# A hybrid attention and delta-rule layer on one core: products of probabilities and v in batches of ready blocks, and a new slab order

## The chip, the core and the metric

The kernel runs on one core of a Trainium2 chip. The core has a matrix engine (TensorE, PE in the profile), a vector engine (VectorE, DVE), a scalar engine (ScalarE, ACT), a general engine (GpSimd, POOL) and a sync engine (SyncE, SP) that issues most DMAs. Each works through its own instructions in order and waits for the others at semaphores. Matmuls read SBUF and write banks of PSUM. The metric is the device time of one execution in microseconds (us): before, the median of 3 runs is 747.47, with 744.84, 747.47 and 747.5.

## The reference

One layer of an encoder over 512 tokens of width 1024, in float32. What matters here:

```
h  = rms_norm(x)                                   # one projection of h for all that follows
q, k = rope(rms_norm(heads)); v = heads            # 8 query heads, 2 key/value heads of 128
s  = q k^T * scale;  pr = softmax(s);  o_att = pr v
y_att = (o_att * silu(az)) @ w_br_att
qkv = silu(short_conv(dq, dk, dv));  o_dn = gated delta rule, chunks of 64, forward and backward
y_dn = (rms_norm(o_dn) * silu(dz)) @ w_br_dn
mix = (sigmoid(gate_att) * y_att + sigmoid(gate_dn) * y_dn) @ w_out
x = x + rms_norm(mix)
x = x + rms_norm(sigmoid(x @ w_ple_gate) * (p @ w_ple_proj))
```

Every large product is computed with both operands split in a high part that the matrix engine takes in one pass and a low rest, and three matmuls (low x high, high x low, high x high) are added up in PSUM.

## The kernel before, in words

**Staging.** The weights come in slabs of 128 x 1024 (512 KB). ACT casts a slab to its high part (`whi`), POOL or DVE subtracts to get the low part (`wlo`; `split`, line 250), and PE runs eight steps of three 128 x 512 matmuls on it (`gemm_t`, lines 549 to 551; `gemm_n` and `gemm_k`, lines 568 to 570 and 586 to 588, for slabs on the moving side). Homes of slabs are two `wraw`, `whi` and `wlo` each, and units `u0` to `u16` lent for a time (`SPARE`). First come the projections of h in the sequence of `ORDER` (dk, dq, dv are the delta rule's; az, dz, gA, gB gates; kv, q0, q1 attention), with the delta rule's two groups of four heads beside them (`chain`), then `ydn` (branch projection of the delta rule), attention, `yatt`, `out0`, `out1`, `pg0`, `pg1`.

**Attention** (`att_heads`, line 1581) is done in two batches g of four heads. For each head and 128 queries PE makes scores (lines 1606 to 1608), DVE their maximum, ACT the exponential with the row's sum, and DVE transposes the result in blocks of 32 into `T` (unit `u0`), so that 16 blocks b of 32 keys lie on 32 partitions each. Then each block is prepared (line 1658: ACT casts the high part, DVE subtracts the low part) into a home of its own: `ring0`, `ring1` (unit `u14`) or one of three `blk` tiles. The products with v (`pv`, line 1641) are twelve matmuls for a block: three split terms times four groups a of 32 partitions, each group on 32 rows of the array with 512 columns, into four banks `po`. PE runs a block's products once more than `AHEAD` = 4 blocks are pending, and the planner may put other parts' matmuls between blocks. The second batch's `att_heads(1)` is started when the first batch's products are done. Afterwards DVE multiplies `po` with the gate, and ACT and POOL or DVE split it (lines 1691 to 1710).

**Planner.** Nothing of the order on the engines is written out by hand. `Flow` (line 36) runs the parts as generators on a clock of assumed durations. A part asks for a home ("get"), a time ("at"), an event ("ev") or PE for a duration ("pe"); of the ready parts the one with the lowest priority number goes on. Other engines' operations are recorded at the first free time that the planner sees for their engine. `W` marks a DVE operation during which the planner leaves POOL idle, too; `split` chooses POOL or DVE for a slab by their planned ends and `COOL` or `HOT`. So a change of a duration, a priority or the sequence in `ORDER` redraws the order of all engines. `PVB` is the assumed duration of a block's products, `VGAP` the distance of the loads of v, `PR` the priorities, `OUT0` the places at which slabs of `out0` are loaded.

**Late stages.** `out1_tail` (line 1867) forms the new x for 128 tokens; its last steps are a DVE product into a `whi` or `wlo` tile and PE's transposes of it (line 1888) for `pg0` and `pg1`.

Of the kernel before, what the change touches and what calls it, by code (L numbers as in the profile page):

```python
# [9 lines left out]
F32 = mybir.dt.float32  # L10
F32R = mybir.dt.float32r
# [24 lines left out]
class Flow:  # L36
# [7 lines left out]
    def __init__(self, slots):  # L44
        self.now = 0.0
        self.eng = {}
        self.slots = {k: [0.0] * n for k, n in slots.items()}
        self.parts = []
        self.later = []
        self.n = 0  # L50
        self.shut, self.link = None, lambda a, b: None

    def spawn(self, gen, prio):
        ev = Event()
        self.n += 1
        self.parts.append([prio, self.n, gen, ("at", 0.0), ev])
        return ev
# [49 lines left out]
    def free(self, tag, t=None):  # L107
        self.slots[tag].append(self.now if t is None else t)
# [15 lines left out]
    def run(self):  # L124
        while self.parts:
            best, soon = None, None
            for p in self.parts:
                r = self.ready(p[3])
                if r is None:
                    continue  # L130
                if r <= self.now + 1e-9:
                    if best is None or p[:2] < best[:2]:
                        best = p
                elif soon is None or r < soon:
                    soon = r
            if best is None:
                if soon is None:
                    raise RuntimeError("stuck: " + ", ".join(f"{p[0]} {p[2].__name__} {p[3][:2]}" for p in self.parts))
                self.now = soon
                continue  # L140
            if best[3][0] == "get":
                s = self.slots[best[3][1]]
                s.remove(min(s))
            self.flush()
            try:
                want = next(best[2])
            except StopIteration as e:
                self.parts.remove(best)
                best[4].set(max(self.now, e.value or 0.0))
                continue  # L150
            if want[0] == "pe":
                self.now += want[1]
                want = ("at", self.now)
            best[3] = want
        self.now = 1e9
        self.flush()


ORDER = """
vec dq1 dk0 dk1 dk3 dq2 dk2 dq3 dq0 dv3 dv1 az0 dq5 dq7 dv2 dq6  # L160
az5 gB7 dk5 az6 dz7 dk4 az2 gA2 dz2 gA4 gA6 dv0 gA7 dq4 dk6 gB4
dk7 gA5 gB3 az4 dz1 dv7 dv4 dz6 dz0 gB0 gB1 kv dv5 dv6 gA0 dz4
gB5 az3 az7 gB2 gA3 dz3 q0 dz5 gB6 q1 gA1 az1 free_h ydn3 ydn4 ydn2
ydn5 heads_on0 ydn6 ydn0 heads_on1 ydn1 ydn7 yatt6 yatt1 yatt5 yatt7 yatt4 yatt2 yatt3 yatt0 out0
out1 pg0 pg1
"""
OUT0 = 'yatt0 yatt3 yatt2 yatt7'
PR = dict(dec=1, dm1=11, y=7, conv=1, gate=3, kv=9, q=5, head=6, ple=7, prep=1, tab=6)
GAP = 0.0
EXPS = 0.32  # L170
SP13 = 480.0
SPARE = ((15, "raw", 7.0, 190.0), (11, "pair", 22.0, 80.0), (12, "pair", 22.0, 80.0), (14, "pair", 279.0, 375.0),
         (13, "pair", 443.0, SP13), (6, "pair", 560.0, 640.0), (14, "raw", 590.0, 640.0))
EOUT = 29.73
WIDE = 2.0
LAND = "c2"
LONG, NEAR = 0.6, 1.5
X_DVE = ()
WARM = 5.5
PVB = 0.695  # L180
VGAP = 2.0
HEADHOT = 1
AHEAD = 4
SPAREMM = 2
W1 = 0
COOL, HOT = 13.37, -0.27


@with_exitstack
def layer(ctx, tc, x, xT, pw0, wp1, wt, wba, wn, rows, qkn, hd16, npost, pnorm, dnorm, cs, out):  # L190
    nc = tc.nc
    pe, act, dve, pool, sync = nc.tensor, nc.scalar, nc.vector, nc.gpsimd, nc.sync

    caps = {"wraw": 2, "whi": 2, "wlo": 2, "f2": 5, "c2": 4, "blk": 3, "gi": 2, "go": 2, "mm": 5, "aux": 3}
    F = Flow({**caps, **{f"u{i}": 1 for i in range(17)}})
    op, free, spawn = F.op, F.free, F.spawn
# [6 lines left out]
    def A(dur, dep, fn, *a, **k):  # L203
        return op("ACT", dur, dep, fn, *a, **k)
# [4 lines left out]
    def W(dur, dep, fn, *a, **k):  # L209

        return op(("DVE", "POOL"), dur, dep, fn, *a, **k)
# [14 lines left out]
    def tile(tag, shape, dt=F32):  # L226
        cnt[0] += 1
        return sb.tile(list(shape), dt, tag=tag, bufs=caps.get(tag, 1), name=f"{tag}_{cnt[0]}")
# [95 lines left out]
    load, ple, late = {}, {}, {}  # L324
# [288 lines left out]
    def gate_job(kind, n):  # L613
        o = yield from gemm_t((kind, n))
        gate_ev[kind, n] = spawn(gate_tail(kind, n, o), PR["gate"])

# [325 lines left out]
    def r32(i):  # L942
        return slice(32 * i, 32 * i + 32)
# [562 lines left out]
    v_ev, V4 = {}, {}  # L1506
# [74 lines left out]
    def att_heads(g):  # L1581
# [6 lines left out]
        T = unit(0, [128, 16, 4, 4, 32])  # L1588
# [6 lines left out]
        def soonest(*tags):  # L1595
            return min(tags, key=lambda n: min(F.slots[n], default=1e9))

        tT = 0.0
        for hb in range(4):
            h = 4 * g + hb  # L1600
            for t in range(NT):
# [17 lines left out]
                tT = V(0.64, te, dve.transpose, T[:, :, hb, t, :], P)  # L1619
# [6 lines left out]
            free(f"u{u}")  # L1626
        if g == 1:
            free("u6")
        yield "ev", v_ev[g]
        yield "ev", q_ev[1]  # L1630
        if g == 1:
            weighed.set(F.now)
        po = []
# [4 lines left out]

        chains[0] += HEADHOT

        def pv(b, p):
            v = V4[g][b // 8][:, b % 8]
            for i, j in ((1, 0), (0, 1), (0, 0)):
                for a in range(4):
                    pe.matmul(po[a], v[r32(a), i, :], p[r32(a), j], start=(b == 0 and i == 1), stop=(b == 15 and i + j == 0))  # L1645
            free(tag[b], F.now + PVB + 0.1)

        yield "get", "u14"
        ring = unit(14, [128, 2, 2, 16, 32], F32R)
        for i in range(2):  # L1650
            F.slots[f"ring{i}"] = [F.now]
        pend, tag = [], {}
        for b in range(16):
            tag[b] = soonest("ring0", "ring1", "blk")
            yield "get", tag[b]
            p = tile("blk", [128, 2, 16, 32], F32R) if tag[b] == "blk" else ring[:, int(tag[b][-1])]
            w = T[:, b].rearrange("p h t q -> p (h t) q")
            tl = W(0.58, A(0.52, tT, act.copy, p[:, 0], w), dve.tensor_sub, p[:, 1], w, p[:, 0].bitcast(F32))
            pend.append((b, p, tl))
            if len(pend) > AHEAD:  # L1660
                b_, p_, t_ = pend.pop(0)
                yield "at", t_ + 0.3
                pv(b_, p_)
                yield "pe", PVB
        free("u0", tl)
        for b_, p_, t_ in pend:
            yield "at", t_ + 0.3
            pv(b_, p_)
            yield "pe", PVB
        for u in (15, 13):  # L1670
            free(f"u{u}")
        chains[0] -= HEADHOT
# [2 lines left out]
        free("u14")  # L1675
        if g == 0:
            v_ev[1] = spawn(v_rows(1), 4)
            spawn(att_heads(1), PR["head"])
        us = ((9, 10), (11, 12))[g]
        for u in us:  # L1680
            yield "get", f"u{u}"
# [9 lines left out]
        for a in range(4):  # L1691
            if g == 0:
                yield "get", "c2"
                y = tile("c2", [128, 16, 32])
                t = V(0.66, max(tz), dve.tensor_mul, y, po[a], at(uz))
# [3 lines left out]
                t = G(1.19, th, pool.tensor_sub, at(ya[g][1]), y, at(ya[g][0]).bitcast(F32))  # L1699
# [4 lines left out]
        if g == 1:  # L1704
            half_ev.set(th + 0.2)
            for a in range(4):
                t = V(0.58, th, dve.tensor_sub, at(ya[g][1]), po[a], at(ya[g][0]).bitcast(F32))
# [318 lines left out]
    dec = spawn(decay(), PR["dec"])  # L2026
# [41 lines left out]
    for j in jobs:  # L2068
        f, a = j[0], tuple(j[1:])
# [86 lines left out]
```

## Time and profile before

| | |
|---|---|
| median of 3 runs | 747.47 us (744.84 to 747.5) |
| profiled execution | 745.96 us |
| its span, first to last instruction | 744.2 us |
| granted TensorE clock, mean | 0.996 |
| PE busy | 729.0 us, 98% |
| DVE, ACT, POOL busy | 495.3, 348.8, 304.1 us |
| DMA moved | 118.49 MB, mean 159 GB/s |
| first batch of products (L1645) | 533.2 to 549.4 us of the span |
| second batch of products | 579.4 to 602.0 us |

The page gives busy time by engine, the chain of work that ended last, and the costliest groups of instructions. A matmul's duration runs from its start to its modelled end and overlaps the next one's; what PE needs for a matmul is the distance from its start to the next start. Waits are put down to the engine and tile whose signal came last. The profile's line numbers are those of the code above.

### The profile page before, as it was taken

What the parts mean: (1) busy time and instruction counts of PE and PEld (TensorE: products, weight loads), DVE (VectorE), ACT (ScalarE), POOL (GpSimd) and SP (SyncE); (2) the same over time, 40 slices, a digit from 0 to 9 for tenths busy, and PEclk for the clock granted to TensorE, in tenths of its full rate; (3) what the DMA queues carried; (4) which work ended last, traced back from release to release, by engine and by line L of the source; (5) the groups of instructions that cost most, each with busy time, mean ns of one, the idle gap of its engine ahead of it and who ended that gap; (6) DMA issues with size and microseconds to landing.
All of it is one profiled execution on the core that took longest, in us unless ns stands there. A gap on an engine that the chain in (4) does not pass through costs nothing.

```text
span 744.2 us, 12250 instructions
## 1 busy us (share of the span) xinstructions
PE 729.0 (98%) x4601; PEld 600.7 (81%) x4601; DVE 495.3 (67%) x912; ACT 348.8 (47%) x647; POOL 304.1 (41%) x292
## 2 busy tenths in 40 slices
PE   8999999999999999999999999999999999999995
PEld 7788888888788988887888988888777578887885
DVE  4688989898776668878734537368878863315434
ACT  6657674553643535425532254335656634322422
POOL 5836494211431444125411257454325218372501
PEclk9999999999999999999999999999999999999998
DMA  8774446966530235647431333475556477461323
GB/s 350 249 235 118 165 136 184 309 196 211 133 99 31 84 130 155 213 157 184 151 107 43 102 112 104 165 184 187 185 129 201 156 264 247 135 216 58 103 69 113
DMA packets 74731, 118.49 MB, mean 159 GB/s; under 512 B 23920, under 2 KB 39216, under 8 KB 74672
## 3 DMA queue, kind: packets, MB, share of 16 engines
q1 hardware_dynamic: 74384, 117.45, 49.6%
q8 instruction: 36, 0.59, 0.3%
q10 hardware_dynamic: 288, 0.26, 0.1%
q14 instruction: 23, 0.19, 0.1%
HBM read 93.41 MB, written 24.28 MB: 158 GB/s over the span
## 4 chain that ended last, share of the span: by engine, by line
PE 80%; DVE 8%; ACT 4%; DMA 3%; POOL 3%; issue 2%; POOLq 0%; DVEq 0%; SPq 0%; ACTq 0%
PE mm L549 14%; PE mm L550 14%; PE mm L551 14%; PE mm L570 4%; PE mm L568 4%; PE mm L569 4%; DVE f L122 3%; PE aux L1645 3%; PE mm L588 2%; PE mm L586 2%; PE mm L587 2%; PE aux L1218 2%; PE aux L1250 2%; PE aux L1236 2%; PE aux L1198 1%
## 5 line engine op out<-in xcount | busy, mean ns | idle before, releaser
L549 PE MATMUL mm<-u,wlo 128*128 128x512 f32 x488 | 197.2, 404 | 1.3 <-POOL wlo L102 0.9
L102 POOL TENSOR_TENSOR wlo<-wraw,whi 128x1024 fp32r<-128x1024 f32 x47 | 112.5, 2394 | 208.3 <-ACT whi L122 197.2
L551 PE MATMUL mm<-u,whi 128*128 128x512 f32 x488 | 190.4, 390 | 0.0
L550 PE MATMUL mm<-u,whi 128*128 128x512 f32 x488 | 190.2, 390 | 0.0
L549 PEld LDWEIGHTS mm<-u,wlo 128*128 128x128 f32 x488 | 91.8, 188 | 23.8 <-issue 4.0
L551 PEld LDWEIGHTS mm<-u,whi 128*128 128x128 f32 x488 | 91.6, 188 | 19.6
L550 PEld LDWEIGHTS mm<-u,whi 128*128 128x128 f32 x488 | 91.9, 188 | 16.4
L122 ACT CAST whi<-wraw 128x1024 fp32r<-128x1024 f32 x62 | 64.9, 1047 | 68.7 <-PE mm L551 28.3
L122 DVE SCALAR_TENSOR_TENSOR f<-mm,cw,f 128x510 f32<-128x510 f32 (+1 forms) x96 | 71.4, 745 | 6.6 <-ACT f L122 4.1
L568 PE MATMUL mm<-u,u 128*128 128x512 f32 (+1 forms) x136 | 52.0, 382 | 0.0
L570 PE MATMUL mm<-u,u 128*128 128x512 f32 (+1 forms) x136 | 51.3, 377 | 0.0
L569 PE MATMUL mm<-u,u 128*128 128x512 f32 (+1 forms) x136 | 51.2, 377 | 0.0
L102 POOL TENSOR_TENSOR u<-wraw,u 128x1024 fp32r<-128x1024 f32 x17 | 40.6, 2400 | 21.1 <-ACT u L122 21.0
L122 DVE TENSOR_TENSOR u<-aux,u 128x512 f32<-128x512 f32 (+2 forms) x55 | 36.1, 667 | 17.5 <-ACT u L122 11.7
L122 ACT COPY c<-aux 128x512 f32<-128x512 f32 x18 | 10.6, 587 | 48.1 <-DVE f L122 26.0
L586 PE MATMUL mm<-whi,u 128*128 128x512 f32 x80 | 31.8, 398 | 0.0
L588 PE MATMUL mm<-whi,u 128*128 128x512 f32 x80 | 31.2, 390 | 0.0
L587 PE MATMUL mm<-wlo,u 128*128 128x512 f32 x80 | 31.1, 389 | 0.0
L122 ACT ACTIVATE mm<-f 128x512 f32<-128x512 f32 x24 | 14.4, 600 | 32.2 <-DVE f L122 32.0
L570 PEld LDWEIGHTS mm<-u,u 128*128 128x128 f32 x136 | 25.6, 188 | 4.8
L569 PEld LDWEIGHTS mm<-u,u 128*128 128x128 f32 x136 | 25.6, 188 | 4.5
L568 PEld LDWEIGHTS mm<-u,u 128*128 128x128 f32 x136 | 25.6, 188 | 4.4
(286 smaller groups left out, 1499.9 us busy)
## 6 DMA issues: line engine op xcount, KB each, us to landing
wraw<-in_wt_dram SPq DMA_DIRECT2D x58, 512.0 KB, 3.7
wraw<-in_wn_dram SPq DMA_DIRECT2D x24, 512.0 KB, 4.4
u<-in_wt_dram SPq DMA_DIRECT2D x14, 512.0 KB, 5.9
u<-CI SPq DMA_DIRECT2D x16, 256.0 KB, 5.6
u<-VD SPq DMA_DIRECT2D x16, 256.0 KB, 6.8
u<-in_x_dram SPq DMA_DIRECT2D x4, 512.0 KB, 5.9
u<-in_xT_dram SPq DMA_DIRECT2D x4, 512.0 KB, 8.2
eD<-u SPq DMA_DIRECT2D x8, 256.0 KB, 5.0
```

Source lines behind the costliest of these rows:

```text
L102: ins = fn(*a, **k)
L122: fn(*a, **k)
L549: pe.matmul(o, lo[:, k, :], mh(k), start=(k == 0), stop=False)
L550: pe.matmul(o, hi[:, k, :], ml(k), start=False, stop=False)
L551: pe.matmul(o, hi[:, k, :], mh(k), start=False, stop=(k == 7))
L568: pe.matmul(o, b, hi, start=(i == 0), stop=False)
L569: pe.matmul(o, a, lo, start=False, stop=False)
L570: pe.matmul(o, a, hi, start=False, stop=(i == 7))
L586: pe.matmul(o[t], b, hi, start=(k == 0), stop=False)
L587: pe.matmul(o[t], a, lo, start=False, stop=False)
L588: pe.matmul(o[t], a, hi, start=False, stop=(k == 7))
L1645: pe.matmul(po[a], v[r32(a), i, :], p[r32(a), j], start=(b == 0 and i == 1), stop=(b == 15 and i + j == 0))
```

## The change

1. The products of a batch begin when up to `BATCH` = 4 blocks are ready (or all that are pending), and go on with the next block without giving PE away if that block is ready by the planner's clock; a visit that comes back from other work is planned `TURN` = 0.3 longer. `Flow.steps` counts PE requests, so that a part sees whether another one had PE in between. `AHEAD` goes.
2. A block may also live in two `c2` tiles, when at least two are free: with four `c2` tiles that makes seven homes instead of five.
3. `att_heads(1)` is started when the first batch's last block is prepared, and `v_ev` is polled, since the second batch's loads of v may not be spawned yet.
4. `ORDER`, `OUT0`, the priorities `PR`, `VGAP` (2.0 to 1.2), `EOUT` and `HOT` have new values.

```
@@ ORDER and constants
-vec dq1 dk0 dk1 dk3 dq2 dk2 dq3 dq0 dv3 dv1 az0 dq5 dq7 dv2 dq6
...
-ydn5 heads_on0 ydn6 ydn0 heads_on1 ydn1 ydn7 yatt6 yatt1 yatt5 yatt7 yatt4 yatt2 yatt3 yatt0 out0
+dq2 dk1 dk2 dk0 dq3 dk3 dq0 dq1 dv3 az4 dv1 dv2 dk4 az0 dq7 dq5
...
+ydn5 heads_on0 ydn1 ydn7 ydn0 ydn4 yatt1 yatt6 yatt2 yatt4 yatt0 yatt3 yatt5 heads_on1 yatt7 out0
-OUT0 = 'yatt0 yatt3 yatt2 yatt7'
-PR = dict(dec=1, dm1=11, y=7, conv=1, gate=3, kv=9, q=5, head=6, ple=7, prep=1, tab=6)
+OUT0 = 'yatt3 yatt4 yatt0 yatt5'
+PR = dict(dec=3, dm1=1, y=9, conv=1, gate=9, kv=3, q=3, head=9, ple=9, prep=1, tab=9)
-EOUT = 29.73
+EOUT = 29.88
-VGAP = 2.0
+VGAP = 1.2
-AHEAD = 4
+BATCH, TURN = 4, 0.3
-COOL, HOT = 13.37, -0.27
+COOL, HOT = 13.37, 0.47
@@ Flow.run
             if want[0] == "pe":
                 self.now += want[1]
+                self.steps += 1
@@ att_heads
+        while g not in v_ev:
+            yield "at", F.now + 1.0
         yield "ev", v_ev[g]
...
-        pend, tag = [], {}
-        for b in range(16):
-            tag[b] = soonest("ring0", "ring1", "blk")
-            yield "get", tag[b]
-            p = tile("blk", [128, 2, 16, 32], F32R) if tag[b] == "blk" else ring[:, int(tag[b][-1])]
-            w = T[:, b].rearrange("p h t q -> p (h t) q")
-            tl = W(0.58, A(0.52, tT, act.copy, p[:, 0], w), dve.tensor_sub, p[:, 1], w, p[:, 0].bitcast(F32))
-            pend.append((b, p, tl))
-            if len(pend) > AHEAD:
-                b_, p_, t_ = pend.pop(0)
-                yield "at", t_ + 0.3
-                pv(b_, p_)
-                yield "pe", PVB
-        free("u0", tl)
-        for b_, p_, t_ in pend:
-            yield "at", t_ + 0.3
-            pv(b_, p_)
-            yield "pe", PVB
+        def room():
+            ways = [(min(F.slots[n], default=1e9), n) for n in ("ring0", "ring1", "blk")]
+            if len(F.slots["c2"]) > 1:
+                ways.append((sorted(F.slots["c2"])[1], "c2"))
+            return min(ways)
+
+        pend, b, seen_ = [], 0, -1
+        while b < 16 or pend:
+            at, tag = room()
+            if b < 16 and (at <= F.now or not pend):
+                yield "get", tag
+                if tag == "c2":
+                    yield "get", "c2"
+                    p = [tile("c2", [128, 16, 32], F32R) for _ in range(2)]
...
+                tl = W(0.58, A(0.52, tT, act.copy, p[0], w), dve.tensor_sub, p[1], w, p[0].bitcast(F32))
+                pend.append((b, p, tag, tl))
+                b += 1
+                if b == 16:
+                    free("u0", tl)
+                    if g == 0:
+                        spawn(att_heads(1), PR["head"])
+                continue
+            n = min(BATCH, len(pend)) if F.steps != seen_ else 1
+            if pend[n - 1][3] + 0.3 > F.now:
+                yield "at", pend[n - 1][3] + 0.3
+                if F.steps != seen_:
+                    continue
+            b_, p, tag, _ = pend.pop(0)
...
+            took = PVB + (TURN if F.steps != seen_ else 0.0)
+            for _ in range(2 if tag == "c2" else 1):
+                free(tag, F.now + took + 0.1)
+            yield "pe", took
+            seen_ = F.steps
...
         if g == 0:
             v_ev[1] = spawn(v_rows(1), 4)
-            spawn(att_heads(1), PR["head"])
```

What this does to the order of the engines, at three places. In the rows, `mm` and `aux` are PSUM banks, `blk`, `u` and `c` tiles in SBUF, and lines from 1650 on stand 19 lines later in the change's code (L1645 becomes L1684; L549 to L551 become L550 to L552).

PE, first batch of products, before: the end of the first block's products, a step of another projection (bank `mm_5268`), and the begin of the second block's.

```order
L1645 MATMUL aux_5250<-blk_5255,u_643_4807 128x512
L1645 MATMUL mm_5251<-blk_5255,u_643_4807 128x512
L1645 MATMUL aux_5252<-blk_5255,u_643_4807 128x512
L1645 MATMUL mm_5253<-blk_5255,u_643_4807 128x512
L549 MATMUL mm_5268<-u_573_4360,wlo_5208 128x512
L550 MATMUL mm_5268<-u_574_4361,whi_5207 128x512
L551 MATMUL mm_5268<-u_573_4360,whi_5207 128x512
L1645 MATMUL aux_5250<-blk_5256,u_643_4807 128x512
L1645 MATMUL mm_5251<-blk_5256,u_643_4807 128x512
```

The same place in the change: the last matmul of that projection (bank `mm_5275`), the first block's first group, and below the border between the first and the second block.

```order
L552 MATMUL mm_5275<-u_573_4369,whi_5205 128x512
L1684 MATMUL aux_5258<-blk_5263,u_644_4820 128x512
L1684 MATMUL mm_5259<-blk_5263,u_644_4820 128x512
L1684 MATMUL aux_5260<-blk_5263,u_644_4820 128x512
L1684 MATMUL mm_5261<-blk_5263,u_644_4820 128x512
...
L1684 MATMUL mm_5261<-blk_5263,u_644_4820 128x512
L1684 MATMUL aux_5258<-blk_5264,u_644_4820 128x512
L1684 MATMUL mm_5259<-blk_5264,u_644_4820 128x512
```

The projection's steps moved ahead of the products. Before, the first batch's 192 matmuls stand in runs of 12, 12, 12, 12 and 144; in the change in one run of 192. The second batch's stand before in eleven runs of 12 and one of 60, and in the change in runs of 60 and 132, with six steps of three between. Between the last scores and the first products are 39 matmuls before and 42 in the change in the first batch, 30 and 39 in the second.

DVE, first batch, before: the subtractions for the blocks (the first operand is T) and the slab splits among them.

```order
L122 SCALAR_TENSOR_TENSOR go_5209<-go_5209,mm_5210 128x512
L97 TENSOR_TENSOR blk_5255<-u_672_4979,blk_5255 128x512
L97 TENSOR_TENSOR blk_5256<-u_672_4979,blk_5256 128x512
L97 TENSOR_TENSOR blk_5257<-u_672_4979,blk_5257 128x512
L97 TENSOR_TENSOR u_720_5254<-u_672_4979,u_720_5254 128x512 x2
L97 TENSOR_TENSOR wlo_5267<-wraw_5159,whi_5266 128x1024
L97 TENSOR_TENSOR blk_5315<-u_672_4979,blk_5315 128x512
L97 TENSOR_TENSOR blk_5334<-u_672_4979,blk_5334 128x512
L97 TENSOR_TENSOR blk_5355<-u_672_4979,blk_5355 128x512
L97 TENSOR_TENSOR wlo_5375<-wraw_5265,whi_5374 128x1024
```

And in the change:

```order
L122 STREAM_TRANSPOSE rrow_120<-rinv 128x32
L97 TENSOR_TENSOR blk_5263<-u_671_4987,blk_5263 128x512
L97 TENSOR_TENSOR blk_5264<-u_671_4987,blk_5264 128x512
L97 TENSOR_TENSOR blk_5265<-u_671_4987,blk_5265 128x512
L97 TENSOR_TENSOR c_725_5267<-u_671_4987,c_724_5266 128x512
L97 TENSOR_TENSOR u_720_5262<-u_671_4987,u_720_5262 128x512 x2
L97 TENSOR_TENSOR wlo_5274<-wraw_5198,whi_5273 128x1024
L97 TENSOR_TENSOR c_735_5328<-u_671_4987,c_734_5327 128x512
L97 TENSOR_TENSOR wlo_5326<-wraw_5272,whi_5325 128x1024
L97 TENSOR_TENSOR blk_5357<-u_671_4987,blk_5357 128x512
```

Six blocks instead of five come ahead of the first slab split, one gate operation less stands ahead of them, and the second split comes behind the seventh block instead of the eighth.

PE, output projection `out1`, before: the matmuls of the second 128 tokens (bank `mm_6638`) around the first transposes of the first 128 tokens' new x.

```order
L568 MATMUL mm_6638<-u_868_6484,u_825_6169 128x512
L569 MATMUL mm_6638<-u_869_6485,u_824_6168 128x512
L570 MATMUL mm_6638<-u_868_6484,u_824_6168 128x512
L1888 MATMUL aux_6661<-ident,whi_6596 128x128 x4
L568 MATMUL mm_6638<-u_866_6482,u_829_6188 128x512
```

And in the change:

```order
L569 MATMUL mm_6659<-u_882_6516,u_841_6209 128x512
L570 MATMUL mm_6659<-u_883_6517,u_840_6208 128x512
L571 MATMUL mm_6659<-u_882_6516,u_840_6208 128x512
L1907 MATMUL aux_6688<-ident,whi_6617 128x128 x4
L569 MATMUL mm_6659<-u_882_6516,u_841_6209 128x512
```

Before, 15 matmuls of that bank stand ahead of the transposes, in the change 21.

More of the change, by code (lines that the diff above doesn't have):

```diff
@@ L49, in __init__ @@
         self.later = []
-        self.n = 0
+        self.n = self.steps = 0
         self.shut, self.link = None, lambda a, b: None
@@ L159 @@
 ORDER = """
-vec dq1 dk0 dk1 dk3 dq2 dk2 dq3 dq0 dv3 dv1 az0 dq5 dq7 dv2 dq6
-az5 gB7 dk5 az6 dz7 dk4 az2 gA2 dz2 gA4 gA6 dv0 gA7 dq4 dk6 gB4
-dk7 gA5 gB3 az4 dz1 dv7 dv4 dz6 dz0 gB0 gB1 kv dv5 dv6 gA0 dz4
-gB5 az3 az7 gB2 gA3 dz3 q0 dz5 gB6 q1 gA1 az1 free_h ydn3 ydn4 ydn2
-ydn5 heads_on0 ydn6 ydn0 heads_on1 ydn1 ydn7 yatt6 yatt1 yatt5 yatt7 yatt4 yatt2 yatt3 yatt0 out0
+dq2 dk1 dk2 dk0 dq3 dk3 dq0 dq1 dv3 az4 dv1 dv2 dk4 az0 dq7 dq5
+vec az2 dk5 az6 gA7 dq6 gA4 dz2 gA2 gB4 dz7 dv0 gB6 dq4 gA6 dk6
+dk7 gB3 gA5 dz4 az5 dv6 dv4 dz6 gB7 gB0 kv dv5 gA0 dv7 dz0 az7
+dz1 az3 gA3 gA1 gB1 dz3 q0 gB2 dz5 q1 gB5 az1 free_h ydn2 ydn6 ydn3
+ydn5 heads_on0 ydn1 ydn7 ydn0 ydn4 yatt1 yatt6 yatt2 yatt4 yatt0 yatt3 yatt5 heads_on1 yatt7 out0
 out1 pg0 pg1
 """
-OUT0 = 'yatt0 yatt3 yatt2 yatt7'
-PR = dict(dec=1, dm1=11, y=7, conv=1, gate=3, kv=9, q=5, head=6, ple=7, prep=1, tab=6)
+OUT0 = 'yatt3 yatt4 yatt0 yatt5'
+PR = dict(dec=3, dm1=1, y=9, conv=1, gate=9, kv=3, q=3, head=9, ple=9, prep=1, tab=9)
 GAP = 0.0
@@ L1639, in att_heads @@
         chains[0] += HEADHOT
[L1641 to L1646, printed above, removed]
         yield "get", "u14"
@@ L1665, in att_heads @@
-        free("u0", tl)
-        for b_, p_, t_ in pend:
-            yield "at", t_ + 0.3
-            pv(b_, p_)
-            yield "pe", PVB
+        def room():
[11 more added lines that the diff above has]
+                    p = [tile("c2", [128, 16, 32], F32R) for _ in range(2)]
+                else:
+                    p = tile("blk", [128, 2, 16, 32], F32R) if tag == "blk" else ring[:, int(tag[-1])]
+                    p = [p[:, 0], p[:, 1]]
+                w = T[:, b].rearrange("p h t q -> p (h t) q")
+                tl = W(0.58, A(0.52, tT, act.copy, p[0], w), dve.tensor_sub, p[1], w, p[0].bitcast(F32))
[12 more added lines that the diff above has]
+            b_, p, tag, _ = pend.pop(0)
+            v = V4[g][b_ // 8][:, b_ % 8]
+            for i, j in ((1, 0), (0, 1), (0, 0)):
+                for a in range(4):
+                    pe.matmul(po[a], v[r32(a), i, :], p[j][r32(a)], start=(b_ == 0 and i == 1), stop=(b_ == 15 and i + j == 0))
+            took = PVB + (TURN if F.steps != seen_ else 0.0)
[3 more added lines that the diff above has]
+            seen_ = F.steps
```

## The prediction

> **What bounds the kernel now.** I read the page first, its busy time and the shares of the chain that ended last.
>
> ```profile
> PE 729.0 (98%) x4601; PEld 600.7 (81%) x4601; DVE 495.3 (67%) x912; ACT 348.8 (47%) x647; POOL 304.1 (41%) x292
> PE 80%; DVE 8%; ACT 4%; DMA 3%; POOL 3%; issue 2%; POOLq 0%; DVEq 0%; SPq 0%; ACTq 0%
> ```
>
> TensorE (PE) is busy 98% of the span and makes 80% of the chain. Next I read the waits of PE alone:
>
> ```profile
> PE aux L1888 <- DVE whi L97: 1.4, 1, 1.4
> PE mm L549 <- POOL wlo L102: 0.9, 1, 0.9
> ...
> PE aux L1645 <- DVE u L97: 0.2, 1, 0.2
> ```
>
> All its rows together are 7.3 us. So there is little waiting to win. What can shrink is the time that PE spends busy without progress, and that is seen only in the timeline, where matmuls overlap and the distance between starts is the cost. First three matmuls of an ordinary projection step, then a stretch in which the products of probabilities and v (L1645) alternate with such steps, then the end of the long run of products in the first batch. The columns are start, duration, engine, line, operation and tiles:
>
> ```profile
> 571.97 0.39 PE L549 MATMUL mm<-u,wlo 128*128 128x512 f32 x1
> ...
> 572.65 0.39 PE L549 MATMUL mm<-u,wlo 128*128 128x512 f32 x1
> ...
> 581.29 0.50 PE L1645 MATMUL aux<-blk,u 32*128 32x512 f32 x3
> ...
> 582.19 0.50 PE L549 MATMUL mm<-u,wlo 128*128 128x512 f32 x1
> 582.53 0.40 PE L550 MATMUL mm<-u,whi 128*128 128x512 f32 x1
> 582.76 0.39 PE L551 MATMUL mm<-u,whi 128*128 128x512 f32 x1
> 583.08 0.50 PE L1645 MATMUL aux<-blk,u 32*128 32x512 f32 x3
> ```
>
> ```profile
> 547.26 0.40 PE L1645 MATMUL aux<-u,u 32*128 32x512 f32 x2
> ...
> 547.94 0.40 PE L1645 MATMUL aux<-u,u 32*128 32x512 f32 x2
> ...
> 548.62 0.40 PE L1645 MATMUL aux<-blk,u 32*128 32x512 f32 x2
> ```
>
> A projection step of three matmuls takes 572.65 - 571.97 = 0.68 us. A block of products (three groups of four matmuls on 32 rows each) takes 0.68 inside a run (547.26, 547.94, 548.62). Where the two alternate, the block takes 582.19 - 581.29 = 0.90 and the step 583.08 - 582.19 = 0.89, 1.79 together where 1.36 would do. So each visit of PE to the products costs **0.43 us** for turning to them and back, with no idle time shown: the first matmul behind a turn lasts 0.50 instead of 0.39.
>
> **The change, part by part.** *Fewer visits.* By the order of PE, the first batch of 16 blocks has five visits before (1, 1, 1, 1 and 12 blocks), and the second twelve (eleven of one block, then 5). In the change the first is one run of 16, the second 5 and 11 with six steps between: 17 visits become 3. No matmul is added or removed on PE. 14 x 0.43 = **6.0 us** saved. The whole stretches agree:
>
> ```profile
> 540.32 0.49 PE L1645 MATMUL aux<-u,u 32*128 32x512 f32 x1
> ...
> 544.63 0.50 PE L1645 MATMUL aux<-u,u 32*128 32x512 f32 x1 [0.22 <-DVE u L97]
> ...
> 549.42 0.50 PE L1606 MATMUL mm<-u,u 128*128 128x512 f32 x1
> ...
> 579.40 0.50 PE L1645 MATMUL aux<-blk,u 32*128 32x512 f32 x3
> ...
> 601.95 1.19 PE L1776 MATMUL mm<-u,whi 128*128 128x512 f32 x4
> ```
>
> From 579.40 to 601.95 are 22.55 us, for 16 blocks and 29 other matmuls that need 16 x 0.68 + 29 x 0.227 = 17.5; the 5.0 left are twelve turns of 0.43, less what falls outside the ends.
>
> *The gap in the first run.* The run from 540.32 to 549.42 takes 9.10 us for 12 blocks: 8.2, a turn's half (0.2), and 0.7 us lost around the wait at 544.63. Does a run of 16 starve more? The last scores, the rows of the block's two preparers, and a slab's split that stands between them:
>
> ```profile
> 523.99 0.39 PE L1608 MATMUL mm<-u,u 128*128 128x512 f32 x1
> ```
> ```profile
> 529.54 1.66 ACT L122 CAST blk<-u 128x512 fp32r<-128x512 f32 x3 [0.78 <-DVE u L122]
> ```
> ```profile
> 531.14 1.89 DVE L97 TENSOR_TENSOR blk<-u,blk 128x512 fp32r<-128x512 f32 x3
> ...
> 534.15 1.22 DVE L97 TENSOR_TENSOR wlo<-wraw,whi 128x1024 fp32r<-128x1024 f32 x1
> ```
>
> ScalarE (ACT) casts a block in about 0.52 and VectorE (DVE) subtracts in about 0.60, below PE's 0.68. In the order of DVE two slab splits (1.2 each) and one gate operation (0.6) stand among the 16 subtractions: 16 x 0.60 + 3.0 = 12.6 us, against 16 x 0.68 = 10.9 on PE. PE starts behind: from the last scores to the products it has 42 matmuls (9.5 us), where the trace has the first subtraction done 531.8 - 524.2 = 7.6 us after the last scores; so some four blocks are ready, and the seven homes hold them. The second of the slab's casts takes the room that PE frees with its last matmul before the run, so ACT is held until then. Followed through, every block is ready about 0.6 us or more before PE wants it. A collision with GpSimd (POOL; below) would eat that. Of the 0.7 I take 0.4 as gained; the ends are 0.7 and -1.3.
>
> The second batch has more cover: 39 matmuls (8.9 us) ahead instead of 30, and six steps (4.1 us) between its visits. The slab that PE waited 0.93 us for just ahead of it has the same place in POOL's order, so I leave that wait as it is.
>
> *Output projection.* Four rows from the place where PE waits longest:
>
> ```profile
> 674.17 0.39 PE L570 MATMUL mm<-u,u 128*128 128x512 f32 x1
> 675.94 0.66 PE L1888 MATMUL aux<-ident,whi 128*128 128x128 f32 x4 [1.39 <-DVE whi L97]
> ```
> ```profile
> 672.97 2.37 POOL L102 TENSOR_TENSOR u<-wraw,u 128x1024 fp32r<-128x1024 f32 x1
> ```
> ```profile
> 673.03 2.85 DVE L97 SCALAR_TENSOR_TENSOR whi<-u,fs,whi 128x512 f32<-128x512 f32 x1 [0.42 <-POOL fs L306]
> ...
> 680.96 0.75 DVE L97 SCALAR_TENSOR_TENSOR whi<-u,fs,whi 128x512 f32<-128x512 f32 x1 [0.33 <-POOL fs L306]
> ```
>
> DVE's product takes 2.85 us beside POOL's subtraction and 0.75 without it, and the transposes wait: 675.94 - 674.17 is 1.77 for a matmul of 0.23. In the change 21 matmuls instead of 15 stand before the first transposes: 6 x 0.227 = 1.36 of cover. I take **1.4 us**; the ends are 0 (the collision comes later and longer) and 1.5.
>
> *At nothing.* The homes from c2 add no instruction (8 subtractions write c2, 8 fewer blk and u); the second batch's scores are recorded sooner, but stand directly behind the last product on PE before and after; DMAs are 397 on SP's queue before and after. All of it is hidden by PE's other matmuls; if v's loads, now spread at 1.2 instead of 2.0, came late, the second batch would wait, but the scores and the 39 matmuls stand between.
>
> *The redrawn order.* 72 slabs come in another sequence, with other priorities. No row of before shows the new waits. PE's waits without the start (1.4) and the transposes (1.4) are 4.5 us; the new order could lose most of them or have twice as many: -3 to +4.5. I charge 1.0, one wait like that on wlo.
>
> Sum: 6.0 + 0.4 + 1.4 - 1.0 = **6.8 us** off a span of 744.2, 737.4. The profiled execution took 745.96, so 739.2 by it; against the median of the three runs, 747.47 (744.84 to 747.5), 740.7. I forecast 740.
>
> **The rivals.** *Blocks set the pace.* From the first subtraction (row 578.97) to the last (598.43 + 0.69) the second batch takes 20.1 us:
>
> ```profile
> 578.97 1.90 DVE L97 TENSOR_TENSOR blk<-u,blk 128x512 fp32r<-128x512 f32 x3 [0.38 <-ACT blk L122]
> ...
> 598.43 0.69 DVE L97 TENSOR_TENSOR blk<-u,blk 128x512 fp32r<-128x512 f32 x1 [0.88 <-ACT blk L122]
> ```
> ```profile
> 597.77 0.62 ACT L122 CAST blk<-u 128x512 fp32r<-128x512 f32 x1 [0.95 <-PE mm L1645]
> ```
>
> If that is DVE's own pace, the second batch keeps its end and loses its 10 x 0.43 = 4.3: 744.3. Against it: the idle time before the last of them ends with ACT, and ACT's cast had waited for PE to free a home (the third row); with seven homes and no turns both come sooner.
>
> *The block itself costs 0.90 outside its run.* Then only the steps recover, 14 x 0.21 = 2.9 instead of 6.0, and the time is 743. The rows at 547.26 to 548.62 speak against it. The Trainium skill (TensorE: Matmul & The Clock Gate, section "Why this matters for your kernels") has four such 32-row matmuls run 3.07 times as fast as one after the other, not four times; by that a block would cost an estimated 3 x 4 / 3.07 x 0.227 = 0.89 us wherever it stands. The run's 0.68 differs, and the measurement decides.
>
> *Slabs take the gain back.* PE comes 6 us sooner to the branch and output projections, and if their slabs come when they came before, the time is 746 to 747. Against it:
>
> ```profile
> POOL wlo L102 <- ACT whi L122: 203.6, 33, 30.2
> ACT whi L122 <- PE mm L551: 36.0, 17, 3.9
> ```
>
> POOL waits for ACT, and ACT for PE to free a slab: they come sooner if PE does.
>
> *Slower: the second delta-rule chain ends late.* The ydn projections need it. Its last pieces and the first ydn matmul (the third row):
>
> ```profile
> 480.36 0.60 PE L1312 MATMUL mm<-ident,u 128*128 128x128 f32 x4
> ```
> ```profile
> 482.41 0.69 DVE L122 TENSOR_TENSOR u<-mm,u 128x512 fp32r<-128x512 f32 x1 [0.66 <-ACT u L122]
> ```
> ```profile
> 506.54 0.39 PE L549 MATMUL mm<-u,wlo 128*128 128x512 f32 x1
> ```
>
> The cover is 506.54 - 483.1 = 23.4 us, 0.7 less in the new order (three matmuls). A chain that is late by more than 22.7 us costs one for one; from 22.7 + 6.8 + 3.7 = 33 us late on, the kernel is slower: 36 us would give 754. Against it: the chain's first solve stands 7 rows earlier on PE.
>
> **How the numbers follow.** Half a per cent, 3.7 us, is about what can be told from no change: faster is below 743.7, slower above 751.2. Chances: the forecast 0.74 (own range 737 to 743.5); blocks set the pace 0.09 (744); the block's own cost 0.02 (743); slabs take it back 0.07 (746.5); the chain 0.04 (754); and 0.04 that the redrawn order also removes 3 us or more of waits (736). Faster: 0.74 x 0.97 + 0.04 + half of 0.11 = 0.82; slower 0.05; same 0.13. The range runs from 736 to 745.5: it takes in the sum's ends (4.5 more waits and a run that starves) and leaves out the last two rivals.
>
> **What would show it.** Right: three visits to the products in the timeline, starts of blocks 0.68 apart, the stretch of the first batch about 11 us long, of the second 15 with its six steps; the wait at the first output transposes below 0.5. Wrong: idle PE with DVE as releaser inside a run of products; waits for wlo ahead of the branch projections; visits gone, yet the span within 3 us of before, which would put the gain's loss in the redrawn order.

## The result, and the profile after

| | before | after |
|---|---|---|
| median of the executions beside each other | 747.1 us (744.84 to 747.5) | 737.57 us (737.14 to 738.01) |
| ratio | | 0.9879, 95% interval 0.9858 to 0.99 |
| profiled execution | 745.96 us | 737.61 us |
| its span | 744.2 us | 735.9 us |
| granted TensorE clock | 0.996 | 0.998 |

The changed kernel is faster by 9.5 us by the medians and by 8.35 us between the two profiled executions. The page of the changed kernel, busy time and shares of the chain that ended last:

```profile
PE 723.1 (98%) x4601; PEld 604.4 (82%) x4601; DVE 492.7 (67%) x911; ACT 350.3 (48%) x658; POOL 304.0 (41%) x291
PE 81%; DVE 5%; issue 5%; ACT 3%; POOL 3%; DMA 2%; POOLq 0%; SPq 0%; DVEq 0%; ACTq 0%
```

PE runs the same 4601 matmuls and is busy 5.9 us less: most of the gain was busy time, as the prediction had it. PE's waits are now, all of them:

```profile
PE mm L2036 <- POOL ident masks.py:199: 1.4, 1, 1.4
PE aux L1129 <- issue: 1.1, 2, 0.6
PE aux L1219 <- ACT c L122: 0.5, 1, 0.5
PE mm L550 <- POOL wlo L102: 0.5, 1, 0.5
PE mm L878 <- DVE partk L122: 0.4, 1, 0.4
PE mm L672 <- POOL u L102: 0.4, 1, 0.4
PE mm L550 <- DVE wlo L97: 0.3, 1, 0.3
PE mm L1340 <- DVE u L97: 0.2, 1, 0.2
```

They sum to 4.8 us, where before they were 7.3. The row of 1.4 us at the output's transposes is gone, and the wait for `wlo` ahead of the second batch is 0.5 in place of 0.9.

Where along the span is the difference? I take the same places on PE in both traces. Two of them in the kernel before, the first score and the last matmul:

```profile
502.65 0.40 PE L1606 MATMUL mm<-u,u 128*128 128x512 f32 x1
...
736.44 0.28 PE L570 MATMUL mm<-u,u 128*128 128x256 f32 x1
```

And in the changed kernel the first score, the start and the end of the first batch's products (L1684, the end by the score behind them), the two visits of the second batch with the steps between, the first matmul behind them, and the last matmul:

```profile
502.68 0.40 PE L1607 MATMUL mm<-u,u 128*128 128x512 f32 x1
...
535.90 0.49 PE L1684 MATMUL aux<-blk,u 32*128 32x512 f32 x1
...
547.47 0.50 PE L1607 MATMUL mm<-u,u 128*128 128x512 f32 x1
...
579.02 0.50 PE L1684 MATMUL aux<-blk,u 32*128 32x512 f32 x3
...
582.66 0.50 PE L550 MATMUL mm<-u,wlo 128*128 128x512 f32 x1
...
586.97 0.50 PE L1684 MATMUL aux<-c,u 32*128 32x512 f32 x3
...
594.69 0.50 PE L1811 MATMUL mm<-u,wlo 128*128 128x512 f32 x1
...
728.09 0.28 PE L571 MATMUL mm<-u,u 128*128 128x256 f32 x1
```

| stretch on PE | before | after | difference |
|---|---|---|---|
| up to the first score | 502.65 | 502.68 | 0.0 |
| first score to the end of the first batch | 46.77 | 44.79 | -2.0 |
| from there to the end of the second batch | 52.53 | 47.22 | -5.3 |
| from there to the last matmul | 134.49 | 133.40 | -1.1 |

The new slab order, which redraws all that lies ahead of the first score, is worth nothing there that can be told: the first score comes at 502.5 to 503.4 us in the ten traces with the new order, and at 502.7, 503.1 and 504.5 in the three with the old one. There are three visits: 547.47 - 535.90 = 11.57 us for 16 blocks, 582.66 - 579.02 = 3.64 for 5 and 594.69 - 586.97 = 7.72 for 11; five and eleven blocks at 0.684 are 3.42 and 7.52, and 0.21 us is left over in each, half a turn. No PE row in the second batch's visits names a releaser.

At the output transposes, the rows of the changed kernel on PE, and then on DVE, ACT and POOL:

```profile
668.72 0.39 PE L571 MATMUL mm<-u,u 128*128 128x512 f32 x1
668.95 0.60 PE L1907 MATMUL aux<-ident,whi 128*128 128x128 f32 x4
```
```profile
666.22 0.75 DVE L97 SCALAR_TENSOR_TENSOR whi<-u,fs,whi 128x512 f32<-128x512 f32 x1 [0.42 <-POOL fs L307]
```
```profile
669.40 1.05 ACT L122 CAST u<-wraw 128x1024 fp32r<-128x1024 f32 x1 [4.33 <-DMA wraw<-in_wn_dram]
```
```profile
670.52 2.40 POOL L102 TENSOR_TENSOR u<-wraw,u 128x1024 fp32r<-128x1024 f32 x1 [4.34 <-ACT u L122]
```

The transposes follow the last matmul at once. The product took 0.75 us: POOL's subtraction, which had stood beside it, begins at 670.52 only, since its slab came late by DMA and ACT's cast with it. So the collision did not happen here, and the longer cover (668.95 - 666.22 = 2.7 us from the product's start to the transposes) was not put to the test.

### The profile page after: what moved, and what is told of

It reads as the page before. It is cut to its first block, busy times and chain, and to the rows that moved or that the text cites. A ratio compares the mean times of both kernels' runs of the same rounds, so it can differ in the third digit from the quotient of the medians.

```text
span 735.9 us, 12258 instructions
## 1 busy us (share of the span) xinstructions
PE 723.1 (98%) x4601; PEld 604.4 (82%) x4601; DVE 492.7 (67%) x911; ACT 350.3 (48%) x658; POOL 304.0 (41%) x291
## 4 chain that ended last, share of the span: by engine, by line
PE 81%; DVE 5%; issue 5%; ACT 3%; POOL 3%; DMA 2%; POOLq 0%; SPq 0%; DVEq 0%; ACTq 0%
PE mm L550 14%; PE mm L552 14%; PE mm L551 14%; PE mm L569 4%; PE mm L571 4%; PE mm L570 4%; PE mm L589 3%; PE mm L587 3%; PE mm L588 3%; DVE f L122 2%; PE aux L1251 2%; PE aux L1219 2%; PE aux L1237 2%; POOL u L102 2%; PE aux L1684 2%
## 5 line engine op out<-in xcount | busy, mean ns | idle before, releaser
L550 PE MATMUL mm<-u,wlo 128*128 128x512 f32 x488 | 196.3, 402 | 0.8 <-POOL wlo L102 0.5
L102 POOL TENSOR_TENSOR wlo<-wraw,whi 128x1024 fp32r<-128x1024 f32 x45 | 107.6, 2393 | 204.8 <-ACT whi L122 196.9
L552 PE MATMUL mm<-u,whi 128*128 128x512 f32 x488 | 190.6, 391 | 0.0
L551 PE MATMUL mm<-u,whi 128*128 128x512 f32 x488 | 190.4, 390 | 0.0
L550 PEld LDWEIGHTS mm<-u,wlo 128*128 128x128 f32 x488 | 91.8, 188 | 20.5 <-POOL wlo L102 1.7
L552 PEld LDWEIGHTS mm<-u,whi 128*128 128x128 f32 x488 | 91.6, 188 | 19.6
L551 PEld LDWEIGHTS mm<-u,whi 128*128 128x128 f32 x488 | 91.9, 188 | 17.0
L122 ACT CAST whi<-wraw 128x1024 fp32r<-128x1024 f32 x60 | 62.6, 1047 | 61.1 <-PE mm L552 18.2
L102 POOL TENSOR_TENSOR u<-wraw,u 128x1024 fp32r<-128x1024 f32 x19 | 45.4, 2401 | 15.3 <-ACT u L122 15.2
```

The source lines that it names most:

```text
L102: ins = fn(*a, **k)
L122: fn(*a, **k)
L550: pe.matmul(o, lo[:, k, :], mh(k), start=(k == 0), stop=False)
L551: pe.matmul(o, hi[:, k, :], ml(k), start=False, stop=False)
L552: pe.matmul(o, hi[:, k, :], mh(k), start=False, stop=(k == 7))
```

## The experiments

Each ratio below is to the kernel before, in executions beside it on the same chip; the medians of the kernel before in these sets are 747.2, 747.0 and 746.4 us.

### What does a turn cost?

First the direct test: into the first run of the changed kernel, between each two blocks, one matmul more, once on all 128 rows and once on 32. Neither leaves anything out; the extra bank isn't read.

```diff
+        if g == 0:
+            yield "get", "mm"
+            spare = bank("mm")
...
+            if g == 0 and b_ < 15:
+                pe.matmul(spare, v[:, 0, :], p[0], start=True, stop=True)
```

> The changed kernel with fifteen matmuls more: in the first batch, between each two of the sixteen blocks of the run, one matmul of all 128 rows (128x512) into a bank that nothing reads. Nothing is left out. In the changed kernel's trace the run's group of four 32-row matmuls takes 0.228 us and a 128x512 matmul of all rows between its own kind about the same, so the fifteen cost 15 x 0.227 = 3.4 us for their work alone. Theory (it is the turn between 32-row and 128-row matmuls that costs, 0.43 us there and back): the run is cut into sixteen visits, so 15 x (0.227 + 0.43) = 9.9 us are added: 747.4 from 737.5, about the time of the kernel before. Rival (a visit's price lay in what the old loop did between the blocks, waits or the steps' own cost, and not in the turn): 3.4 us are added: 741.

The control has this in its place:

```diff
+                pe.matmul(spare, v[r32(0), 0, :], p[0][r32(0)], start=True, stop=True)
```

> The control to the fifteen 128-row matmuls: the same fifteen, at the same places and into the same spare bank, but on 32 rows (32x512), as the run's own matmuls are. No turn is made. Theory of the turn: what a matmul costs and no more, at most 15 x 0.227 = 3.4 us, less if it runs beside its neighbours on other rows: 738 to 741. Rival (any foreign matmul that breaks the blocks apart, with its other bank, costs the same): as much as the 128-row ones.

Measured: **746.77 us** with the 128-row matmuls (ratio 0.9992, 0.9982 to 1.0003), **740.33** with the 32-row ones (0.9901, 0.9883 to 0.9919); both are what the theory of the turn expected. The difference is 6.44 us, 0.43 for each of fifteen. In the trace of the first, the extra matmuls and the products around them:

```profile
537.35 0.50 PE L1690 MATMUL mm<-blk,u 128*128 128x512 f32 x1
537.78 0.50 PE L1688 MATMUL aux<-blk,u 32*128 32x512 f32 x1
...
538.68 0.49 PE L1690 MATMUL mm<-blk,u 128*128 128x512 f32 x1
539.10 0.50 PE L1688 MATMUL aux<-blk,u 32*128 32x512 f32 x1
...
540.00 0.49 PE L1690 MATMUL mm<-blk,u 128*128 128x512 f32 x1
```

and in that of the control, one group of its extra matmuls, seven of the fifteen with the first and the last among them (columns: durations least, median, greatest in ns; first and last start):

```profile
L1690 PE MATMUL mm<-blk,u x7: 384/384/393, 536.7 to 549.4; 32*128 32x512 f32 x7
```

With turns a block and its extra matmul come every 538.68 - 537.35 = 1.33 us, without every (549.4 - 536.7) / 14 = 0.91. The same number of matmuls, the same blocks, the same run: 0.42 us is the price of turning to 128 rows and back, half of it on each side (the extra matmul holds PE for 537.78 - 537.35 = 0.43 and not 0.23, and the block 0.90 and not 0.68). With the fifteen turns (6.4) and the own work of fifteen matmuls (2.8, from 737.57 to 740.33) the changed kernel has about the time of the kernel before.

What happens at a turn can be read from PE's weight loads (PEld) in the kernel before, the first row in an ordinary step, the second at a turn:

```profile
572.42 0.19 PEld L549 LDWEIGHTS mm<-u,wlo 128*128 128x128 f32 x1
...
582.19 0.19 PEld L549 LDWEIGHTS mm<-u,wlo 128*128 128x128 f32 x1 [0.36 <-issue]
```

The first is the load for the matmul that starts at 572.65, and runs beside the matmul before it. The second starts together with its own matmul (582.19), and so it is at all 17 turns to the products and all 17 back in this trace: at a turn the load's 0.19 us is not hidden. That this is what makes up the half turn of 0.21 is read from the rows; no run tried it.

The Trainium skill (TensorEngine Tiling (Array Packing), section "Key Properties") says that a change of the tiling mode drains TensorE; it gives no price, and 0.42 us for there and back is what it is worth in these traces.

### The loop alone, and the order alone

The kernel before with the new loop of products (and its homes in `c2`), old `ORDER` and constants:

```diff
-            if len(pend) > AHEAD:
...
+            n = min(BATCH, len(pend)) if F.steps != seen_ else 1
```

> The kernel before with the new product loop alone (batches, seven homes, the second batch's scores started sooner); slab order, priorities and constants stay as before. Its products stand in 3 visits (16; 6 and 10 blocks) instead of 17. If the turns make the gain: 14 x 0.43 = 6.0 us less than before, 741 us, and up to 1 us less still where the gap in the first run goes. If the redrawn slab order makes it: within 1 us of before, 747.

The new `ORDER` and constants with the old loop (`AHEAD` = 4 kept):

```diff
-vec dq1 dk0 dk1 dk3 dq2 dk2 dq3 dq0 dv3 dv1 az0 dq5 dq7 dv2 dq6
...
+dq2 dk1 dk2 dk0 dq3 dk3 dq0 dq1 dv3 az4 dv1 dv2 dk4 az0 dq7 dq5
```

> The change's slab order, priorities, out0 places, v spacing and HOT with the product loop of before (AHEAD = 4, five homes). Its products stand in 15 visits. If the turns make the gain: 2 x 0.43 = 0.9 us less than before, and what the new order saves at the output transposes (1.5), so 744.5 to 746. If the order makes it: 738 to 740.

Measured: the loop alone **741.11 us** (0.992, 0.989 to 0.9951), 6.1 less than before; the order alone **743.76** (0.9947, 0.9928 to 0.9966), 3.4 less. The first is what was expected of the turns, the second below the 744.5 to 746 expected of them, by the wait for `wlo` (below) that the expectation left out. The loop's part is the size of the prediction's turns, but not as purely as it looks: its output product did not collide either (0.75 us), which should have brought 1.4 more, and new waits took that back. PE's waits of the loop alone from 490 to 582 us:

```profile
PE aux L1607 <- ACT u L122: 1.3, 1, 1.3
PE mm L550 <- POOL wlo L102: 1.2, 2, 0.7
```

The order alone has 15 visits in place of 17 (0.9 us), no collision, and of the wait for `wlo` ahead of the second batch 0.2 us are left:

```profile
PE mm L549 <- POOL wlo L102: 0.2, 1, 0.2
```

0.9 + 1.4 + 0.7 = 3.0 of its 3.4. So the two parts add up to the whole change (6.1 + 3.4 = 9.5) as far as their intervals tell, some 2.3 and 1.4 us either way, though each contains the missing collision, and the loop alone pays for it elsewhere.

### Are the homes in `c2` needed?

```diff
-            if len(F.slots["c2"]) > 1:
+            if False:
```

> The changed kernel without the homes in c2: five homes as before, visits unchanged (16; 5 and 11 blocks). If PE is fed in time with five homes as well, within 0.5 us of the change, 737.6. If the two more homes keep the long runs fed: idle PE with DVE as releaser inside the runs, 1 to 3 us in all, 739 to 741.

Measured: **738.22 us** (0.9874, 0.985 to 0.9897), 0.65 above the changed kernel's 737.57 and between the two expectations. These sets don't tell it from nothing: by the ratio to the kernel before it is no slower than the changed kernel (0.9879). The trace shows a part of it: the first run now has a wait that the changed kernel doesn't have.

```profile
541.45 0.50 PE L1684 MATMUL aux<-blk,u 32*128 32x512 f32 x1 [0.22 <-DVE blk L97]
```

The run from 536.61 to 548.64 takes 12.03 us, 0.46 more than with seven homes. The run still has 16 blocks and the second batch 5 and 11. The homes feed the run; they don't make it.

### The collision of DVE's product with POOL's subtraction

The kernel before, in which POOL's slab subtractions late in the plan wait for the DVE product ahead of them (three such waits). No engine's order changes.

```diff
-            if ins is not None and self.shut and self.shut[1] is not None and t - self.shut[0] < NEAR:
+            if ins is not None and self.shut and self.shut[1] is not None and t - self.shut[0] < (NEAR if t < 640.0 else 8.0):
```

> The kernel before with the same order on every engine; only behind 640 us of the plan GpSimd's slab subtractions wait for the DVE product that the plan has ahead of them (3 such waits). If the collision of the two is what holds the first output transposes: the product takes 0.75 instead of 2.85 us and the time falls by 1.5 us, to 745.6. If the transposes wait for something else: no change, 747.

Measured: **745.25 us** (0.9971, 0.9958 to 0.9983), 2.0 less than before where 1.5 was expected; the interval takes in 1.3 to 3.1. In its trace the product, the subtraction behind it and the transposes:

```profile
674.59 0.75 DVE L97 SCALAR_TENSOR_TENSOR whi<-u,fs,whi 128x512 f32<-128x512 f32 x1 [0.42 <-POOL fs L306]
```
```profile
675.48 2.41 POOL L102 TENSOR_TENSOR u<-wraw,u 128x1024 fp32r<-128x1024 f32 x1 [0.92 <-issue]
```
```profile
675.72 0.39 PE L570 MATMUL mm<-u,u 128*128 128x512 f32 x1
675.96 0.49 PE L1888 MATMUL aux<-ident,whi 128*128 128x128 f32 x3
```

The product is back at 0.75 us, POOL starts when it ends, and the transposes don't wait. From the end of the second batch to the last matmul the trace has 132.91 us against 134.49: 1.6 is the collision. (Its profiled span is the one of the kernel before all the same, 744.2, since this execution came to the first score 1.9 us later; the medians decide.) The Trainium skill (SBUF — State Buffer, section "SBUF: two separate sides") has an exclusive lock on the ports that VectorE and GpSimd share: whoever starts first keeps them for its whole instruction, and a VectorE operation with two SBUF inputs waits. The trace agrees to 0.2 us: POOL at 672.97 for 2.37 us, DVE's product from 673.03 to 675.88, by the lock to 675.34 + 0.75 = 676.09.

### When may a run start?

`BATCH` of 1 and of 6 in place of 4:

```diff
-BATCH, TURN = 4, 0.3
+BATCH, TURN = 1, 0.3
```

> The changed kernel with one block ready in place of four ahead of a run: by its order seven visits in place of three (7 and 9; 5, 5, 2, 1 and 8 blocks). Theory of the turn: four more turns, 4 x 0.43 = 1.7 us more, 739.2. Rival (what made the loop faster is that a run goes on while the next block is ready, and a start with four ready adds nothing; turns cost less than the visits of the kernel before suggest): 737.5, no change.

> The changed kernel with six blocks ready in place of four ahead of a run; by its order this makes two visits in place of three (16 and 16, where the changed kernel has 16, 5 and 11), and the six steps of the last slab go ahead of the second run. Theory of the turn: 0.43 us less, 737.1 from 737.5, hardly to be told from no change. Rival (the second run, now sixteen blocks without a pause, waits for its blocks, which the six steps between the two visits had given time to be made): sixteen blocks by VectorE at some 0.9 us each are 14.4 us against 11 us of the run less six blocks ahead, so up to 0.5 us of waits, and no gain.

Measured: **740.56 us** for one block (0.9906, 0.9891 to 0.9921) and **741.01** for six (0.9919, 0.9903 to 0.9935). Both are 3 us and more above the changed kernel, and neither theory had that: two visits come out slower than three. The expectation for one block also miscounted: by the trace there are six visits (7 and 9 blocks; 5, 2, 1 and 8), three more than in the changed kernel and not four, so 1.3 us and not 1.7. The waits of PE tell why. With one block:

```profile
PE aux L1907 <- DVE whi L97: 1.4, 1, 1.4
```

With six blocks:

```profile
PE aux L1907 <- DVE whi L97: 1.4, 1, 1.4
...
PE mm L1811 <- ACT u L122: 1.0, 1, 1.0
...
PE aux L1684 <- DVE blk L97: 0.4, 1, 0.4
```

The row at the output's transposes is the one that PE had waited for longest in the kernel before: the redrawn order put POOL's subtraction beside DVE's product again. In the kernel with one block:

```profile
667.43 2.85 DVE L97 SCALAR_TENSOR_TENSOR whi<-u,fs,whi 128x512 f32<-128x512 f32 x1 [0.42 <-POOL fs L307]
```
```profile
667.37 2.37 POOL L102 TENSOR_TENSOR u<-wraw,u 128x1024 fp32r<-128x1024 f32 x1
```

So a third set takes the collision away from both, and from the changed kernel, with the same line as in the kernel before:

> The kernel with one block ready ahead of a run (seven visits), with one thing changed: POOL's subtraction of a slab waits, late in the plan, for VectorE's product ahead of it, as in the kernel before with that wait. No engine's order changes. In the trace of the kernel with one block the first product of the output projection lasts 2.85 us beside POOL's subtraction, and PE waits 1.4 us at the transposes. Theory (the 3.0 us that it stands above the changed kernel are four turns, 1.7, and this collision, 1.4): 740.56 - 1.4 = 739.2, and the wait at the transposes is gone. Rival (a start with one block makes the runs starve, and the collision is hidden anyway): 740.5, with the 1.4 us lost elsewhere.

> The same one change made to the kernel with six blocks ready ahead of a run (two visits), in whose trace the same collision stands. Theory: the 3.4 us above the changed kernel are the collision (1.4), the wait inside the run for a block (590.05, about 0.6) and one for ACT's cast behind it (1.0), less a turn of 0.43; so 741.0 - 1.4 = 739.6. Rival (two visits are worth their turn, and all of the loss is the collision): 737.

> The changed kernel with the same one change. In its trace the collision does not stand: the product lasts 0.75 us, since POOL's slab came late by DMA (4.33 us waited by the cast for wraw). Theory: no change where that DMA is late in every execution, 737.6; if the collision comes back in some executions, the wait takes it out of those, and the median falls by less than 0.5. Rival (holding POOL back delays the last slabs for PE): up to 1.5 us more, 739.

Measured: **738.60 us** (0.989, 0.9868 to 0.9911), **739.62** (0.9901, 0.988 to 0.9922) and **737.77** (0.9876, 0.9855 to 0.9897). The wait is gone in both, and 2.0 and 1.4 us with it by the medians. These lie in two sets, though, in which the kernel before has 747.0 and 746.4; by the ratios to it the gain is 1.2 and 1.3 us. In the traces the stretch from the end of the second batch to the last matmul shrinks by 1.60 and 1.62 us (137.68 to 136.08 and 134.89 to 133.27), as it did by 1.58 in the kernel before. The changed kernel, which has no collision, stays where it was. With one block and no collision:

```profile
667.16 0.75 DVE L97 SCALAR_TENSOR_TENSOR whi<-u,fs,whi 128x512 f32<-128x512 f32 x1 [0.42 <-POOL fs L307]
```

What is left above the changed kernel is 0.8 to 1.0 us for three visits more and 1.8 to 2.1 for one visit less. Three turns are 1.3; 0.4 of it comes back in the first batch, where the changed kernel's run of 16 loses 11.57 - 16 x 0.684 - 0.21 = 0.4 us to blocks that come late, and the two runs of 7 and 9 (5.00 and 6.37 us) lose none. 1.3 - 0.4 = 0.9 is what was measured.

The 0.4 does not lie in the length of the run. With six blocks ready the first run, also of 16 blocks, goes from 535.91 to 547.03, 11.12 us, and loses none. What differs is a gate product on POOL. In the changed kernel it stretches three of DVE's subtractions from 1.89 to 2.99 us (rows in the next section). With six blocks ready and POOL not held, the subtractions keep their time and POOL's product, 1.3 us when alone, is the one that waits:

```profile
539.74 1.89 DVE L97 TENSOR_TENSOR blk<-u,blk 128x512 fp32r<-128x512 f32 x3
```
```profile
538.57 7.81 POOL L102 TENSOR_TENSOR u<-u,gi 128x512 f32<-128x512 f32 x1 [5.79 <-DMA gi<-SR]
```

With one block ready the subtractions are stretched as well (2.98), and there the steps between the two visits cover it.

For six blocks, with POOL held at the output, three of PE's waits are not in the changed kernel:

```profile
PE mm L1811 <- ACT u L122: 1.0, 1, 1.0
PE aux L1684 <- DVE blk L97: 0.6, 1, 0.6
...
PE aux L1684 <- DVE c L97: 0.4, 1, 0.4
```

The 0.4 stands in the first run (at 540.85), where the gate product stretches one subtraction from 0.69 to 1.78; this run takes 11.83 us, 0.3 more than the changed kernel's. The 0.6 stands in the second run (at 591.08), which has no steps to split it: 12.05 us in place of 16 x 0.684 + 0.21 = 11.15, so 0.9 lost, twice the turn that it saves. The 1.0 comes behind it, where ACT is late with its next work. 0.9 + 1.0 + 0.3 less a turn of 0.43 are 1.8 of the 1.8 to 2.1. No kernel here beats the changed one.

## Why the prediction was right

The forecast was 740.0 us with a range of 736 to 745.5 and 0.82 for faster (its own terms add up to 0.81); 737.57 came out, so the side and the range were right and the forecast 2.4 us too high. Step by step, in the span of the profiled executions:

- **Fewer visits: 6.0.** The step held. From the first batch's end to the second's, 5.3 us are gone. Two matmuls moved behind the second batch (150 others stand between the batches' ends where there were 152; 0.45), the wait for `wlo` gave 0.46 (0.93 to 0.47; below), and 4.4 remain for ten visits, 0.44 each. The first batch gave 2.0, of which four visits are 1.7. The price read from rows of 0.90 and 0.89 against 0.68 was confirmed by its own experiment, 0.42 in the trace and 0.43 in the time.
- **The gap in the first run: 0.4.** It held: 2.0 less 1.7 is 0.3, and the run still loses 0.4 of what had been 0.7. The collision with POOL that was named as a danger did happen here, in a place that cost little. DVE's three subtractions beside POOL's gate product in the changed kernel:

```profile
539.35 2.99 DVE L97 TENSOR_TENSOR blk<-u,blk 128x512 fp32r<-128x512 f32 x3
```
```profile
538.42 2.16 POOL L102 TENSOR_TENSOR u<-u,gi 128x512 f32<-128x512 f32 x1 [6.05 <-DVE c L97]
```

Three take 1.89 elsewhere. Most of the 1.1 us come out of the blocks that were ready ahead of PE, and 0.4 reach PE: where DVE is not delayed, with six blocks ready, the run loses none.

- **Output projection: 1.4.** The size was right: the 1.1 us of the last stretch and the 0.45 that moved into it make 1.54, and taking the collision away shortened the same stretch by 1.6 in three pairs of traces. The way was not the one told, so that the size came out is in part luck. The prediction had the product still slow and covered by six more matmuls; in fact it was fast, because POOL's slab came late. That the cover would have done it too, the trace doesn't contradict (2.7 us from product to transposes against 2.85 for a slow product), but no run tried it.
- **At nothing: homes, sooner scores, DMAs.** The homes measured at 0.65 us at most, 0.46 in the run: a small gain in the trace, since without them the run starves a little, though the times alone don't tell it from nothing. The sooner scores are nothing: with the start of `att_heads(1)` at its old place, the order of every engine's instructions is the same, row for row.
- **The redrawn order: -1.0.** This term failed, in size and sign. Up to the first score the redrawn order cost 0.0, and the one wait on `wlo` that the prediction left as it was fell from 0.9 to 0.5 us. Ahead of the first score PE's waits changed places (0.6 us more at L1129, 0.5 less at L1340), and no large one is new. With 0.5 in place of -1.0 the sum is 8.3, which is the 8.35 of the profiled executions.
- The rest of the distance is in the bases: the profiled execution of before (745.96) lies 1.1 us below its own median, that of after (737.61) at its median, so by the medians the gain is 9.5.

Of the rivals, the pace of the blocks did not hold in the changed kernel (the second batch lost all of its turns' time), but it takes over where the second batch is not split: with six blocks ready its one run of 16 waits 0.4 us for blocks, and 0.6 with POOL held. That a block costs 0.90 by itself is excluded by the control, where sixteen blocks with fifteen extra matmuls keep 0.91 for both together. The estimate of 0.89 from the Trainium skill (TensorE: Matmul & The Clock Gate, section "Why this matters for your kernels") falls with it: a group of four 32-row matmuls takes 0.228 us here, as much as a single one adds in the control (0.91 - 0.684 = 0.23). The slabs did come sooner with PE (the last stretch did not grow), and the second delta-rule chain was not late: PE's waits from 500 to 604 us hold one row of 0.5, on `wlo`.

## What to carry to other kernels

PE can be busy 98% of the time and still lose 7 us (17 visits at 0.43): look at the distance between starts where matmuls of one tile shape alternate with those of another, price a turn, and collect the work so that there are few turns. Collect only as much as its feeders can hold: a run that outlasts the blocks made ahead waits for them, and the six steps between two visits of 5 and 11 blocks are worth more than the turn that they cost (0.9 us against 0.43). Where a planner redraws the whole order, look in every variant's profile for collisions in places that weren't touched before a difference is put down to the edit; here two parameters looked 3 us worse, and about half of that, 1.6, was one DVE product standing beside one POOL subtraction.

## What the runs showed of the hardware that was not expected

- The collision of DVE's product with POOL's subtraction came whole or not at all: in the thirteen traces the first product of the output projection lasts 2.85 us (before, and with one and with six blocks) or 0.75 (all others), and nothing between. The changed kernel escapes it because a cast waits 4.33 us for its slab's DMA. Holding POOL for some 0.9 us cost nothing that the times show in the three kernels in which it held POOL at this product; in the changed kernel the product was long done.
- The delay can fall on either engine. POOL's gate product, 1.3 us when alone, lasted 7.81 us (538.57 to 546.38) with six blocks ready, while DVE had one operation behind the other until 545.24; in other traces the same product cost DVE 1.1 us and took 1.4 to 3.3 itself.
- A turn costs the same 0.42 us for a single 128-row matmul among products on 32 rows as for a whole visit (0.43 and 0.44): both sides pay half. At each turn the weight load starts with its own matmul, and not beside the one before.
